# First stage of a decoder layer: six split and three raw weight parts, and the memory's values over 512 columns

## The chip, the core and the metric

The kernel runs on one NeuronCore of a Trainium2 chip. The metric is the device time of one execution in microseconds (us). The core's engines are PE (matrix products and transposes), DVE (vector), ACT (scalar and activation), POOL and SP; SP computes nothing and issues most of the DMA transfers, which 16 DMA engines carry out. Every engine, SP too, takes its instructions strictly in the order in which they stand in its queue.

## The reference

One decoder layer: a token-mixing sub-layer (RWKV-7 time mixing and a sparse attention, merged by gates), a cross-attention into 256 memory tokens, and a gated MLP, each followed by a LayerNorm. The parts that matter here are the input projection, the compression of the attention's keys and values, and the memory's keys and values:

```python
proj = x @ w_in[l]                       # x (1024, 1024)
...
def compress(t, pe, w1, w2):             # windows of 32 tokens, stride 16: 63 of them, 2 groups
    blk = t[:, cidx] + pe[None, None, :, None, :]
    blk = blk.transpose(0, 3, 1, 2, 4).reshape(B, G, n_cmp, CMP_BLOCK * dh)
    return jax.nn.gelu(blk @ w1) @ w2    # w1 (2048, 256), w2 (256, 64)
...
def memory_cross_attention(x, mem, wq, wk, wv, wo):
    k = (mem @ wk).reshape(B, M, X_HEADS, X_HEAD_DIM)    # mem (256, 1024), wk and wv (1024, 1024)
    v = (mem @ wv).reshape(B, M, X_HEADS, X_HEAD_DIM)
```

## The kernel before

**Products.** Every float32 operand of a large product is split into a high part and a low rest of the same size (`split`, L199): ACT writes the high part (L200), DVE subtracts it from the source (L201). `mm3` (L194) then makes three products per pair of tiles, high by high, high by low and low by high (L195 to L197), into one PSUM bank.

**Weights.** `wload` (L211) brings a weight block from HBM in parts of at most 1024 elements a partition, which is 512 KB: a part is four row tiles of 256 columns, two of 512, three of 280, eight of 128. For each part SP issues a DMA into a tile `raw` (L224), and `split` writes the tiles `wh` and `wl`. The three tiles of a part come from a pool that `in_turn` picks, in the first stage from `wa` and `p0` by turns. In each of the two pools one raw tile and two pairs of split tiles go round, so two raw and four split parts exist at a time; a new load waits until its raw tile has been split, a new split until the last product on its old tiles is done. From the second stage on only `wa` is left, or `wa` with another pool.

**The first stage** (up to L505) runs in this order: the projection of 512 columns for the selected and window branches' source (`nsa_proj`, L340) with its own weight loads (`wkv_split`, L290), in 8 token tiles of 24 products; the transpose of the memory (`mem_T`); one 256-column block of the memory's keys (`mem_k`, L445) and one of its values (`mem_v`, L455); the windows of the compressed keys; a projection of 280 columns; the compression of the keys (`compress`, L390), two halves of 1024 rows in 2 parts each; the second key and value block, the second one between the windows of the compressed values and their compression; the third key block; the query projection of 512 columns, in 4 parts; the third value block, the fourth key block, the fourth value block. The results of `mem_k` and `mem_v` go to DRAM (`kscr`, `vscr`) and are read again in the cross-attention.

A block of `mem_k` takes 48 products over 256 columns and 2 parts of weights, a block of `mem_v` the same; the keys have the weights as the stationary operand, the values have them as the moving one.

**After it.** `scope0.close()` ends the first stage and frees the pool `p0`; the next pool lies over it, each of its tiles waiting for what lay there. The next stage begins with projections (`prj`, `large` at L512) whose weights come through `wa` alone, beside the recurrence of RWKV, whose order on PE is written out by a small planner. PSUM banks are picked by `in_turn` as well, with one count for each role that goes on from stage to stage.

**Order of the queues.** The framework (Tile) puts the instructions of each engine in order when the kernel is built, by priority (mostly the order of the program) and by when it reckons that each can start, and sets the semaphores. SP's queue holds loads and stores in one order.

Of the kernel before, what the change touches and what calls it, by code (L numbers as in the profile page):

```python
# [10 lines left out]
F32 = mybir.dt.float32  # L11
F32R = mybir.dt.float32r
AF = mybir.ActivationFunctionType
# [5 lines left out]
P = 128  # L19
# [3 lines left out]
HALF = 512  # L23
# [103 lines left out]
def layer_kernel(ctx: ExitStack, tc, I, out, cst):  # L127
# [5 lines left out]
    cur = {}  # L133
    turn = {}

    def opened(name, side="left"):
        st = ExitStack()
        ctx.callback(st.close)
        return st, st.enter_context(tc.tile_pool(name=name, bufs=1, side=side, reuse_waits="tile"))

    def banks(name, **roles):

        if "psum" in cur:
            cur["psum"][0].close()
        st = ExitStack()
        ctx.callback(st.close)
        cur["psum"] = st, st.enter_context(tc.tile_pool(name=name, bufs=1, space=PSUM, reuse_waits="tile"))
        cur["banks"] = roles

    def stt(shape, dt=F32, name="st"):  # L150
        return cur["st"].tile(shape, dt, tag="st", name=name, bufs=cur["nst"])

    def b8(shape, dt=F32, name="b8"):
        if "plan" in cur:
            p, n = cur[next(cur["plan"])]
            return p.tile(shape, dt, tag="a8", name=name, bufs=n)
        return cur["b8"].tile(shape, dt, tag="a8", name=name, bufs=cur["n8"])

    def in_turn(key, xs):
        turn[key] = turn.get(key, -1) + 1  # L160
        return xs[turn[key] % len(xs)]
# [5 lines left out]
    def pg(name="pg"):  # L167
        return bank("g", name)
# [4 lines left out]
    def pst(name="pst"):  # L173
        return bank("t", name)
# [4 lines left out]
    V, S, G, PE, SP = nc.vector, nc.scalar, nc.gpsimd, nc.tensor, nc.sync  # L179

    ident = const.tile([P, P], F32, name="ident")
    _, wa = opened("wa", "right")
    x_scope, xp = opened("xp", "right")
    scope0, p0 = opened("p0")
    cur.update(st=p0, nst=4, b8=p0, n8=3, w=[wa, p0])
    banks("ps0", g=[0, 1, 2, 3], t=[4, 5, 6, 7])

    epsln = const.tile([P, 1], F32, name="epsln")
# [5 lines left out]
    def mm3(o, lh, ll, rh, rl, start, stop):  # L194
        PE.matmul(o, lh, rh, start=start, stop=False)  # L195
        PE.matmul(o, lh, rl, start=False, stop=False)  # L196
        PE.matmul(o, ll, rh, start=False, stop=stop)  # L197

    def split(src, h, l):  # L199
        S.activation(h, src, AF.Copy)  # L200
        V.tensor_sub(l, src, h.bitcast(F32))  # L201

    class W:
        def __init__(self, ku):
            self.ku, self.h, self.l = ku, [], []
# [5 lines left out]
    def wload(pieces, kt=8):  # L211

        n = sum(p.shape[1] for p in pieces)
        w = W(min(kt, WUNIT // n))
        for k0 in range(0, kt, w.ku):
            ku = min(w.ku, kt - k0)
            wp = in_turn("w", cur["w"])
            raw = wp.tile([P, ku, n], F32, tag="raw", bufs=1, name="raw")
            h = wp.tile([P, ku, n], F32R, tag="wh", bufs=2, name="wh")
            l = wp.tile([P, ku, n], F32R, tag="wl", bufs=2, name="wl")  # L220
            o = 0
            for p in pieces:
                m = p.shape[1]
                SP.dma_start(raw[:, :, o:o + m], p[k0 * P:(k0 + ku) * P].rearrange("(k p) n -> p k n", p=P))  # L224
                o += m
            split(raw, h, l)
            w.h.append(h)
            w.l.append(l)
        return w
# [23 lines left out]
    ps = pst("zz")  # L253
# [35 lines left out]

    def wkv_split(u):  # L290
        wp = in_turn("w", cur["w"])
        h = wp.tile([P, 2, HALF], F32R, tag="wh", bufs=2, name="wh")
        l = wp.tile([P, 2, HALF], F32R, tag="wl", bufs=2, name="wl")
        split(wraw[u // 2][:, 2 * (u % 2):2 * (u % 2) + 2], h, l)
        wkv.h.append(h)
        wkv.l.append(l)
# [13 lines left out]
    for gi, grp in enumerate(groups):  # L310
        n = sum(r for _, r in grp)
# [28 lines left out]
    def nsa_proj(cc, n, scale, nb, nh, w=None, ahead=lambda tt: None):  # L340
        w = w or wload([win[:, NSA0 + cc:NSA0 + cc + n]])
        for tt in range(NT):
            ahead(tt)
            ps = pg("np")
            gemmN(ps[:, :n], xT, tt, w, 0, n)
            t = stt([P, HALF], name="nst")
            S.activation(t[:, :n], ps[:, :n], AF.Copy, scale=scale)
            v = t[:, 0:256 * nb].rearrange("p (b h d) -> p b h d", h=4, d=64)[:, :, 0:nh, 0:16]
            for z in range(nb):
                vz = v[:, z]  # L350
                co = cso[:, tt * 16:tt * 16 + 16]
                si = cso[:, P + tt * 16:P + tt * 16 + 16]
                a = p0.tile([P, nh, 16], F32, name="rpa", tag="rpa", bufs=2)
                b = p0.tile([P, nh, 16], F32, name="rpb", tag="rpb", bufs=2)
                G.tensor_tensor(a, vz, bc(co, nh), op=OP.mult)
                G.tensor_tensor(b[:, :, 0:8], vz[:, :, 8:16], bc(si[:, 0:8], nh), op=OP.mult)
                G.tensor_tensor(b[:, :, 8:16], vz[:, :, 0:8], bc(si[:, 8:16], nh), op=OP.mult)
                G.tensor_tensor(vz, a, b, op=OP.add)
            SP.dma_start(rawn[tt * P:(tt + 1) * P, cc:cc + n], t[:, :n])
# [12 lines left out]
    def windows(cc, pe):  # L372
        blk = b8([P, 16, 2, 63], name="blk")
        for g in range(2):
            ev = p0.tile([P, 4, 2, 64], F32, name="ev", tag="ev", bufs=2)
            src = rawn[:, cc + g * 64:cc + g * 64 + 64].rearrange("(b e r) d -> e b r d", b=4, e=P, r=2)
            for b in range(4):
                SP.dma_start(ev[:, b], src[:, b])
            ps = pst("cT")
            for b in range(4):  # L380
                PE.transpose(ps[:, b * P:(b + 1) * P], ev[:, b].rearrange("p r d -> p (r d)"), ident)
            for q in range(2):
                V.tensor_tensor(blk[:, 8 * q:8 * q + 8, g, :], ps[:, 8 * q:8 * q + 504].rearrange("p (i b) -> p b i", b=8),
                                pv[:, col[pe] + 8 * q:col[pe] + 8 * q + 8][:, :, None].to_broadcast([P, 8, 63]), op=OP.add)
        bh = b8([P, 16, 126], F32R, "blkh")
        bl = b8([P, 16, 126], F32R, "blkl")
        split(blk.rearrange("p b g i -> p b (g i)"), bh, bl)
        return bh, bl
# [35 lines left out]
    vscr = drp.tile([MEM, D], F32, name="vscr")  # L424
    memh = p0.tile([P, 8, MEM], F32R, name="memh")
    meml = p0.tile([P, 8, MEM], F32R, name="meml")
# [18 lines left out]
    def mem_k(j):  # L445
        w = wload([I["xa_wk"][0][:, j * 256:(j + 1) * 256]])
        for q in range(2):
            ps = pg("mk")
            for k in range(8):
                mm3(ps[:, :MEM], *w.at(k, q * P, P), memh[:, k], meml[:, k], k == 0, k == 7)  # L450
            t = stt([P, MEM], name="mks")
            S.activation(t, ps[:, :MEM], AF.Copy)
            SP.dma_start(kscr[j * 256 + q * P:j * 256 + q * P + P, :], t)

    def mem_v(j):  # L455
        w = wload([I["xa_wv"][0][:, j * 256:(j + 1) * 256]])
        for mt in range(2):
            ms = slice(mt * P, mt * P + P)
            ps = pg("mv")
            for k in range(8):  # L460
                mm3(ps[:, :256], memh[:, k, ms], meml[:, k, ms], *w.at(k, 0, 256), k == 0, k == 7)
            t = stt([P, 256], name="mvs")
            S.activation(t, ps[:, :256], AF.Copy)
            SP.dma_start(vscr[ms, j * 256:(j + 1) * 256], t)

    def first(tt):
        if tt:
# [22 lines left out]

    mem_T()
    mem_k(0)
    mem_v(0)
    blocks = windows(512, "nsa_pe_k")
    nsa_proj(1024, 280, 1.0, 1, 2)
    compress(*blocks, "nsa_ck_w1", "nsa_ck_w2", True)
    mem_k(1)
    blocks_v = windows(640, "nsa_pe_v")
    mem_v(1)
    compress(*blocks_v, "nsa_cv_w1", "nsa_cv_w2", False)  # L500
    mem_k(2)
    nsa_proj(0, 512, 0.125, 2, 4)
    mem_v(2)
    mem_k(3)
    mem_v(3)  # L505


    gq = list(range(16))
# [441 lines left out]
    with tc.manual_schedule(engines={mybir.EngineType.PE}):  # L950
        while not all(t.done for t in outputs_):
            for tasks in classes:
                t = next((t for t in tasks if not t.done), None)
# [23 lines left out]
    for br, cc in enumerate((768, 1024)):  # L977
# [4 lines left out]
        for j in range(2):  # L982
            ps = pst("kT")
# [15 lines left out]
    for j in range(2):  # L999
        n = (C_ANY - C_CAU) // 2  # L1000
# [283 lines left out]
    w = dict(zip((2, 3), cur["wmb"]))  # L1284
# [20 lines left out]
    for j, k in todo:  # L1305
        g = gate_load(1, k, 0, lambda sh, name: stt(sh, name=name))
        ps = pg("mg")
# [117 lines left out]
    for h in range(XQ):  # L1425
        x_query(h)
        if h == 0:
            kvh = [b8([P, 2048], F32R, f"kvh{i}") for i in range(2)]
            kvl = [b8([P, 2048], F32R, f"kvl{i}") for i in range(2)]
            for i in range(2):  # L1430
                t = b8([P, 2048], name="kvld")
# [34 lines left out]
    for n in (2, 4, 4, 4, 4, 4):  # L1466
# [4 lines left out]
        for i in range(n):  # L1471
            w = wload([wup[:, (f + i) * P:(f + i + 1) * P], wup[:, FF + (f + i) * P:FF + (f + i + 1) * P]])
            gt = b8([P, 2, T], F32R, "gT")
            last = [sm.tile([P, 2], F32, name="cl", tag="cl", bufs=6) for _ in range(2)]
            for half in range(2):
                c = []
                for q in range(2):
                    ps = pg("up")
# [17 lines left out]
        if done:  # L1496
            w = [cols(0), cols(1)]
# [4 lines left out]
        else:  # L1502
            for j in range(2):
                w = cols(j)
# [30 lines left out]
```

## Time and profile before

| | us |
|---|---|
| timed runs, median of 3 | 2225.76 (2222.63 to 2226.09) |
| the profiled execution, its time | 2223.49 |
| its span in the trace | 2221.7 |
| PE busy in the span | 2131.7 (96%) |
| DVE busy | 1232.4 (55%) |
| ACT busy | 889.2 (40%) |

The span runs from the first to the last recorded instruction; what lies around it makes up the difference to the execution's time. The products of a full stream overlap: the profile draws each longer than the distance between two starts.

### The profile page before, as it was taken

The page shows a single profiled execution, that of the slowest core. Times are in us where ns is not written, and L with a number is a line of the kernel's source. Part 1 is how long each engine was busy: PE and PEld are TensorE (multiplying, and loading weights), DVE is VectorE, ACT ScalarE, POOL GpSimd, SP SyncE. Part 2 cuts the span into 40 slices and gives each one's busy share as a digit, 9 for nine tenths or more (in the row PEclk, how much of TensorE's full clock was granted, in tenths as well). Part 3 has the DMA queues.
Part 4 walks back from the last instruction along what each step waited for, and adds up shares of the span by engine and source line. Part 5 has one row for each costly group of instructions (what it writes and reads, how often), then busy time and mean ns, then how long its engine had stood idle before and what let it go on. Part 6 is the DMA issues. An engine that isn't in the chain of part 4 may idle for free.

```text
span 2221.7 us, 31651 instructions
## 1 busy us (share of the span) xinstructions
PE 2131.7 (96%) x12301; PEld 1706.0 (77%) x12301; DVE 1232.4 (55%) x2416; ACT 889.2 (40%) x1441; POOL 475.0 (21%) x544
## 2 busy tenths in 40 slices
PE   9989999999999899999899999999999999999997
PEld 7978777777778667756678877788888888888886
DVE  3422576777652787888656535275444434344447
ACT  3433443544533576776523424142322313132232
POOL 2112231333300244444422101030100101000013
PEclk9999999999999999999999999999999999999999
DMA  6544112121223321112252313111111111111102
GB/s 206 152 150 124 49 24 56 36 52 32 62 59 94 110 66 45 42 45 68 72 189 86 123 38 114 39 39 57 38 48 48 54 42 57 39 57 57 57 29 86
DMA packets 196659, 157.91 MB, mean 71 GB/s; under 512 B 49061, under 2 KB 164766, under 8 KB 196510
## 3 DMA queue, kind: packets, MB, share of 16 engines
q1 hardware_dynamic: 184798, 139.10, 21.2%
q10 hardware_dynamic: 11136, 14.68, 2.0%
q0 software_dynamic: 576, 2.10, 0.3%
q8 instruction: 98, 1.61, 0.3%
q14 instruction: 51, 0.42, 0.1%
HBM read 125.86 MB, written 29.98 MB: 70 GB/s over the span
## 4 chain that ended last, share of the span: by engine, by line
PE 47%; DVE 5%; ACT 2%; DMA 1%; issue 1%; POOL 0%; SPq 0%; ACTq 0%; DVEq 0%; POOLq 0%
PE up L196 7%; PE up L197 7%; PE up L195 7%; PE dn L195 4%; PE dn L197 4%; PE dn L196 4%; PE op L195 2%; PE op L197 1%; PE op L196 1%; PE xq L195 1%; PE xq L196 1%; PE xq L197 1%; DVE acc L1334 1%; ACT acc L1333 1%; DVE bs L1327 1%
## 5 line engine op out<-in xcount | busy, mean ns | idle before, releaser
L200 ACT ACTIVATE wh<-raw 128x1024 fp32r<-128x1024 f32 (+1 forms) x160 | 168.8, 1055 | 474.9 <-PE dn L197 138.1
L201 DVE TENSOR_TENSOR wl<-raw,wh 128x1024 fp32r<-128x1024 f32 (+1 forms) x160 | 198.1, 1239 | 282.5 <-ACT wh L200 281.5
L196 PE MATMUL up<-nTl,wh 128*128 128x512 f32 x704 | 276.5, 393 | 0.0
L197 PE MATMUL up<-nTh,wl 128*128 128x512 f32 x704 | 276.4, 393 | 0.0
L195 PE MATMUL up<-nTh,wh 128*128 128x512 f32 x704 | 276.4, 393 | 0.0
L1458 DVE SCALAR_TENSOR_TENSOR cv<-up,pv,cv 128x511 f32<-128x511 f32 (+1 forms) x176 | 131.5, 747 | 145.4 <-ACT cv L1456 143.4
L1482 POOL TENSOR_TENSOR cv<-cv 128x512 f32<-128x512 f32 x44 | 56.8, 1291 | 630.9 <-DVE cl L1462 413.5
L196 PEld LDWEIGHTS up<-nTl,wh 128*128 128x128 f32 x704 | 132.3, 188 | 29.6
L195 PEld LDWEIGHTS up<-nTh,wh 128*128 128x128 f32 x704 | 132.2, 188 | 29.6
L197 PEld LDWEIGHTS up<-nTh,wl 128*128 128x128 f32 x704 | 132.2, 188 | 29.6
L1106 POOL TENSOR_TENSOR pl<-pe,ph 128x512 fp32r<-128x512 f32 x87 | 114.3, 1317 | 161.3 <-ACT ph L1105 97.3
L195 PE MATMUL dn<-wh,gT 128*128 128x512 f32 x352 | 138.1, 393 | 0.2 <-ACT wh L200 0.2
L197 PE MATMUL dn<-wh,gT 128*128 128x512 f32 x352 | 137.5, 391 | 0.0
L196 PE MATMUL dn<-wl,gT 128*128 128x512 f32 x352 | 136.9, 389 | 0.0
L1493 DVE SCALAR_TENSOR_TENSOR acc<-acc,dn 128x512 f32<-128x512 f32 x96 | 65.5, 686 | 95.5 <-PE dn L197 94.9
L1456 ACT ACTIVATE cv<-up,pv 128x512 f32<-128x512 f32 x88 | 68.5, 778 | 117.2 <-PE up L197 117.2
L195 PE MATMUL gt<-xTh,wh 128*128 128x512 f32 x256 | 113.0, 441 | 0.5 <-DVE nm L1074 0.5
L197 PE MATMUL gt<-xTh,wl 128*128 128x512 f32 x256 | 102.3, 399 | 0.0
L196 PE MATMUL gt<-xTl,wh 128*128 128x512 f32 x256 | 101.9, 398 | 0.0
L1335 POOL TENSOR_TENSOR acc<-acc,lngb 128x1024 f32<-128x1024 f32 x21 | 50.4, 2401 | 206.0 <-DVE acc L1334 129.8
L1105 ACT ACTIVATE ph<-pe 128x512 fp32r<-128x512 f32 (+1 forms) x148 | 90.2, 627 | 6.9 <-POOL macc L1223 4.6
L195 PE MATMUL prj<-xTh,wh 128*128 128x512 f32 x208 | 90.5, 435 | 2.2 <-ACT wh L200 2.2
(365 smaller groups left out, 5092.2 us busy)
## 6 DMA issues: line engine op xcount, KB each, us to landing
raw<-in_ffn_w_up_dram SPq DMA_DIRECT2D x88, 256.0 KB
raw<-in_w_in_dram SPq DMA_DIRECT2D x33, 512.0 KB
raw<-in_ffn_w_down_dram SPq DMA_DIRECT2D x22, 512.0 KB
gscr<-gst ACTq DMA_DIRECT2D x32, 256.0 KB
rawn<-nst SPq DMA_DIRECT2D x16, 256.0 KB
raw<-in_xa_wk_dram SPq DMA_DIRECT2D x8, 512.0 KB
raw<-in_xa_wv_dram SPq DMA_DIRECT2D x8, 512.0 KB
gl<-gscr SPq DMA_DIRECT2D x16, 256.0 KB
```

The source lines that it names most:

```text
L195: PE.matmul(o, lh, rh, start=start, stop=False)
L196: PE.matmul(o, lh, rl, start=False, stop=False)
L197: PE.matmul(o, ll, rh, start=False, stop=stop)
L200: S.activation(h, src, AF.Copy)
L201: V.tensor_sub(l, src, h.bitcast(F32))
L1105: S.activation(h, e, AF.Copy)
L1106: in_turn("l", LTURN)(l, e, h.bitcast(F32), op=OP.subtract)
L1335: (V if tt == NT - 1 else G).tensor_tensor(r[:, c], r[:, c], gb[:, 1, c], op=OP.add)
L1456: S.activation(c, ps, AF.Identity, scale=pc("cw2", ci), bias=pc("ffn_conv_b", ci))
L1458: V.scalar_tensor_tensor(c[:, s:], ps[:, :HALF - s], pc(nme, ci), c[:, s:], op0=OP.mult, op1=OP.add)
L1482: G.tensor_tensor(c[0], c[0], c[1], op=OP.mult)
L1493: V.scalar_tensor_tensor(v, v, 1.0 if f else ALPHA, ps, op0=OP.mult, op1=OP.add)
```

## The change

In the first stage the weight parts are dealt out `p0`, `wa`, `p0` by turns. `p0` holds two raw tiles and four pairs of split tiles, `wa` one and two as before, so that three raw and six split parts exist at a time; `p0` grows by 20 KB a partition. `mem_v` works on 512 columns instead of 256: two calls of 48 products over 512 columns in place of four of 48 over 256, with 4 parts of two row tiles each. The order of the calls becomes: keys 0, keys 1, windows, projection of 280, compression of the keys, values 0, windows, compression of the values, keys 2, query projection, values 1, keys 3.

```diff
-    cur.update(st=p0, nst=4, b8=p0, n8=3, w=[wa, p0])
+    cur.update(st=p0, nst=4, b8=p0, n8=3, w=[p0, wa, p0])
...
+    def depth(wp):
+
+        return (2, 4) if wp is p0 else (1, 2)
...
-            raw = wp.tile([P, ku, n], F32, tag="raw", bufs=1, name="raw")
-            h = wp.tile([P, ku, n], F32R, tag="wh", bufs=2, name="wh")
-            l = wp.tile([P, ku, n], F32R, tag="wl", bufs=2, name="wl")
+            nr, ns = depth(wp)
+            raw = wp.tile([P, ku, n], F32, tag="raw", bufs=nr, name="raw")
+            h = wp.tile([P, ku, n], F32R, tag="wh", bufs=ns, name="wh")
+            l = wp.tile([P, ku, n], F32R, tag="wl", bufs=ns, name="wl")
...
-        h = wp.tile([P, 2, HALF], F32R, tag="wh", bufs=2, name="wh")
-        l = wp.tile([P, 2, HALF], F32R, tag="wl", bufs=2, name="wl")
+        h = wp.tile([P, 2, HALF], F32R, tag="wh", bufs=depth(wp)[1], name="wh")
+        l = wp.tile([P, 2, HALF], F32R, tag="wl", bufs=depth(wp)[1], name="wl")
...
-        w = wload([I["xa_wv"][0][:, j * 256:(j + 1) * 256]])
+        w = wload([I["xa_wv"][0][:, j * HALF:(j + 1) * HALF]])
...
-                mm3(ps[:, :256], memh[:, k, ms], meml[:, k, ms], *w.at(k, 0, 256), k == 0, k == 7)
-            t = stt([P, 256], name="mvs")
-            S.activation(t, ps[:, :256], AF.Copy)
-            SP.dma_start(vscr[ms, j * 256:(j + 1) * 256], t)
+                mm3(ps, memh[:, k, ms], meml[:, k, ms], *w.at(k, 0, HALF), k == 0, k == 7)
+            t = stt([P, HALF], name="mvs")
+            S.activation(t, ps, AF.Copy)
+            SP.dma_start(vscr[ms, j * HALF:(j + 1) * HALF], t)
...
     mem_k(0)
-    mem_v(0)
+    mem_k(1)
     blocks = windows(512, "nsa_pe_k")
     nsa_proj(1024, 280, 1.0, 1, 2)
     compress(*blocks, "nsa_ck_w1", "nsa_ck_w2", True)
-    mem_k(1)
+    mem_v(0)
     blocks_v = windows(640, "nsa_pe_v")
-    mem_v(1)
     compress(*blocks_v, "nsa_cv_w1", "nsa_cv_w2", False)
     mem_k(2)
     nsa_proj(0, 512, 0.125, 2, 4)
-    mem_v(2)
+    mem_v(1)
     mem_k(3)
-    mem_v(3)
```

## Rows read from the trace of the kernel before

**Rows 1.** The page, busy us, share of the span, instructions

```profile
PE 2131.7 (96%) x12301; PEld 1706.0 (77%) x12301; DVE 1232.4 (55%) x2416; ACT 889.2 (40%) x1441; POOL 475.0 (21%) x544
```

**Rows 2.** Windows: length, then busy PE, PEld, DVE, ACT, POOL, clock, DMA share, GB/s

```profile
54.70:70.00 15.30, 15.19 (x126) 14.48 (x125) 7.92 (x15) 7.39 (x12) 1.64 (x8) 1.00 0.61 179
...
95.00:139.50 44.50, 35.06 (x270) 31.59 (x269) 23.52 (x31) 22.49 (x34) 1.62 (x4) 1.00 0.57 174
...
184.70:204.80 20.10, 17.59 (x146) 17.16 (x144) 4.95 (x5) 7.56 (x12) 4.17 (x15) 1.00 0.58 180
...
205.00:2222.00 2017.00, 1942.72 (x11180) 1542.02 (x11179) 1163.39 (x2323) 812.87 (x1328) 433.31 (x374) 0.99 0.21 62
```

**Rows 3.** Timeline of PE: start, length, engine, line, output and inputs, shape

```profile
95.00 0.28 PE L195 MATMUL cm<-wh,blkh 128*126 128x256 f32 x1
...
139.53 0.40 PE L195 MATMUL np<-wh,xTh 128*128 128x512 f32 x1
...
184.72 0.28 PE L195 MATMUL mv<-wh,memh 128*128 128x256 f32 x1
...
190.43 0.29 PE L195 MATMUL mk<-memh,wh 128*128 128x256 f32 x1
...
204.77 0.50 PE L195 MATMUL prj<-xTh,wh 128*128 128x512 f32 x1 [2.20 <-ACT wh L200]
...
206.03 0.50 PE L197 MATMUL prj<-xTh,wl 128*128 128x512 f32 x1 [0.53 <-DVE wl L201]
```

**Rows 4.** Timeline of ACT, evictions of the query projection's last two token tiles

```profile
173.94 0.60 ACT L347 ACTIVATE nst<-np 128x512 f32<-128x512 f32 x1 [4.96 <-PE np L197]
179.50 0.60 ACT L347 ACTIVATE nst<-np 128x512 f32<-128x512 f32 x1 [4.96 <-PE np L197]
```

**Rows 5.** Groups of PE, 95.0 to 139.5: busy, mean ns, idle before

```profile
L381 PE MATMUL cT<-ident,ev 128*128 128x128 f32 x8 | 1.2, 272 | 0.0
...
L409 PE MATMUL kc<-hT,w2s 128*64 128x126 f32 x8 | 0.7, 283 | 0.0
```

**Rows 6.** Waits of PE, 95.0 to 139.5: us in total, times, longest

```profile
PE cm L196 <- DVE wl L201: 3.2, 5, 0.9
...
PE mk L195 <- ACT wh L200: 1.2, 2, 0.7
```

**Rows 7.** Timeline of ACT and SP, one part after another

```profile
123.56 1.06 ACT L200 ACTIVATE wh<-raw 128x1024 fp32r<-128x1024 f32 x1 [2.46 <-DMA raw<-in_nsa_cv_w_dram]
...
119.67 0.37 SPq L224 DMA_DIRECT2D raw<-in_nsa_cv_w_dram  x1
...
122.11 0.37 SPq L224 DMA_DIRECT2D raw<-in_nsa_cv_w_dram  x1
```

**Rows 8.** Timeline of ACT, DVE and SP, the next stage's first weights

```profile
203.66 1.06 ACT L200 ACTIVATE wh<-raw 128x1024 fp32r<-128x1024 f32 x1 [3.47 <-DMA raw<-in_w_in_dram]
...
196.88 1.22 DVE L201 TENSOR_TENSOR wl<-raw,wh 128x1024 fp32r<-128x1024 f32 x1 [1.23 <-ACT wh L200]
...
198.13 0.38 SPq L224 DMA_DIRECT2D raw<-in_w_in_dram  x1
```

**Rows 9.** Waits of SP's queue, 95.0 to 139.5

```profile
SPq L224 <- DVE wl L201: 16.1, 11, 2.4
```

**Rows 10.** Timeline of SP at the end of the 280-column projection

```profile
97.57 0.32 SPq L359 DMA_DIRECT2D rawn<-nst  x1
97.98 0.39 SPq L224 DMA_DIRECT2D raw<-in_xa_wk_dram  x1
```

**Rows 11.** Waits of PE, 205 to the end

```profile
PE x L860 <- DVE ZV L876: 7.6, 12, 1.4
PE z L871 <- ACT SV L867: 5.1, 7, 1.5
...
PE mg L195 <- ACT yh L200: 2.8, 1, 2.8
```

**Rows 12.** Window in the second compression, columns as in group 2

```profile
121.00:132.00 11.00, 6.49 (x44) 5.25 (x43) 4.75 (x4) 4.70 (x6) 0.00 (x0) 1.00 0.63 198
```

## Prediction

> **What bounds the kernel now.** I read the page first, then the table of windows, then the matrix engine's own timeline and waits. On the page the matrix engine PE is busy for 96% of the span [rows 1]; a change pays only where PE stands still or has less to do. The windows say where it stands still in the first stage, which fills the first 205 us of the trace: 44.5 us between 95.0 and 139.5 hold 35.06 us of PE work, and 20.1 us at the end hold 17.59, while the 15.3 us at its head are full but for 0.1; the granted clock is 1.00 in all three [rows 2]. The whole rest, 2017 us, has 1942.72 us of PE work in it and none of the changed lines [rows 2]. So what can be won lies in two places, and the clock is no part of it.
>
> A busy figure hides part of a stall, because one isolated matmul is drawn 0.28 to 0.4 us long while in a full stream the next one starts far earlier. I therefore count starts. 48 products over 256 columns take 190.43 - 184.72 = 5.71 us, 0.119 us each [rows 3]. Over 512 columns one token tile of 24 products takes 5.56 us, 0.232 us each: the eviction of each tile starts that long after the one before [rows 4].
>
> The first place runs from the first product of the first compression (95.00) to the first of the query projection (139.53), 44.53 us [rows 3]. It holds 96 products of the two compressions, 96 of two blocks of keys and 48 of one block of values, all over 256 columns: 240 x 0.119 = 28.6 us. The 28 small transposes and products beside them are drawn at 3.4 us together, four groups from 1.2 down to 0.7 [rows 5]. That makes 32.0 us of work, so 12.5 us of standing still. What PE waits for there is the split weights, the low half wl from DVE above all, and wh from ACT, in five rows from 3.2 down to 1.2 us, 9.4 together [rows 6].
>
> Why they are late: a part of 512 KB is issued by SP at 119.67, the next at 122.11, and the first one's split on ACT starts at 123.56 when it has landed, 3.9 us after its issue [rows 7]. The split takes 1.06 us on ACT and then 1.22 on DVE [rows 7, 8], and only then is the raw tile free for the next load; SP spends 16.1 us of this stretch before its loads on just that release [rows 9]. One raw tile so turns round in 3.9 + 1.06 + 1.22 = 6.2 us, and two of them give a part every 3.1 us. A compression uses up a part in 12 products, 1.43 us; a block of keys in 24, 2.9 us. The supply loses, part after part.
>
> The second place is the end. DVE finishes the low half of a late part at 198.1, SP issues the next stage's first weights at 198.13, they land at 203.66, and PE starts on them at 204.77, with another 0.53 us lost before 206.03 [rows 3, 8].
>
> **The change part by part.** *A third raw part and six split ones.* The parts are dealt out p0, wa, p0 now, and the first stage has 35 of them before and after (8 for the keys, 8 for the values, 4 + 3 + 4 for the projections, 8 for the compressions), so the later stages find the weight turn in the same place. I follow the buffers from the last projection tile before the first compression. Before, one part of the compression was split ahead by then and two lay raw. After, p0 has four split places of which the projection holds two, wa two of which it holds one: three parts are split ahead and three more lie raw, three parts more than before, or 9.3 us of the old supply. Those ready parts carry PE through the first compression (5.7 us) and into the values, and the rest has to arrive meanwhile: with three raw tiles at 6.2 us a turn, one every 2.07 us, against one every 1.4 to 2.9 us that PE uses.
>
> *The other order and the 512 columns.* Between the two compressions there is now one value block of 48 products at 0.232 us, 11.1 us, instead of a key and a value block of 5.7 each. It reads its four parts in its first half; the second half of 5.6 us needs no new part and lets the loads catch up. Following each part (its raw tile free, 3.9 us landing, a split place free, 2.3 us split), I find every later part ready one to six us before its turn; only the third and fourth value parts come out even or up to 1 us late, because their loads queue on SP behind the last projection store, which goes out at 97.57 with a load right behind it at 97.98 [rows 10]. I keep 1.0 us of stall here. The work is 96 + 48 products at 0.119 and 48 at 0.232, and the small ones: 17.1 + 11.1 + 3.4 = 31.7, with the stall 32.7 instead of 44.5: **-11.8 us**.
>
> *The end.* After the query projection come one value block (11.1) and one key block (5.7), 16.8 us, and then the next stage's first product; its third starts 0.5 later, at 17.3 us. Before, 206.03 - 184.72 = 21.3. The last key part is split some 4 us into this stretch, so the next stage's load is issued 13 us before it is wanted and needs 5.5 (198.13 to 203.66) plus the split. I keep 0.5 for the unknown: **-3.5 us**.
>
> *The head.* The second key block stands in the place of a value block with the same 48 products; PE is full there already [rows 2]: 0. *Fewer instructions.* The value products halve from 192 to 96 and their load instructions with them; 2 x 0.119 - 0.232 is 0.006 us each, 0.6 us in all, already inside the two sums. The evictions and stores of values fall from 8 to 4, off PE's path, on ACT and SP, which idle half of these stretches. *Where the bill could come later.* Four accumulations fewer (42 before, 38 after) in the rotation of PSUM banks leave two-bank stages in phase and shift three-bank ones by one; only the merge and what follows it use three. The merge's largest wait on inputs, not banks, is 2.8 us [rows 11], and I take 0, with 3 us either way for the range. p0 grows by 20 KB a partition, and the next stage lays tiles over it, but those are written first some 6 us after its first product: 0.
>
> Sum: -15.3 us. The profiled execution took 2223.5 us (span 2221.7), so 2208.2; the three timed runs lie higher, median 2225.8, and from there it is 2210.5. I say 2211.
>
> **A rule weighed.** In the stretch from 121 to 132 us the 16 DMA engines are busy 0.63 of the time and move 198 GB/s [rows 12], so at full share 314 GB/s and 1.7 us a part; three raw tiles ask for one every 2.07 us, inside that. The Trainium skill, in "DMA: Bandwidth & Descriptors", section "Issuing engines are not separate DMA queues", says that all transfers run on the same 16 engines and interleave with each other. By that rule alone a third load in flight only stretches the other two, and the time would be that of the first rival. The rows speak half against it: the load of 119.67, joined by another 2.4 us later, still landed in 3.9 [rows 7].
>
> **The rivals.** *Contention.* If landing grows with the loads in flight, 3.9 becomes 5.85, a turn 8.1, a part comes every 2.7 us. From 1 us after the first compression's start twelve parts have still to be loaded (the last of the query projection is wanted 32.4 us after that start): 1 + 12 x 2.7 + 2.3 = 35.7, 3.3 us of stall: gain 12, 2214. For it: two raw tiles alone keep the engines busy for 0.63 of the time, stores and all; against: a third one at the same rate asks for no more than they have left [rows 12].
>
> *Only the head start counts.* The third raw tile does nothing that lasts, because SP's queue (loads behind stores) or ACT's (splits behind evictions) keeps the old pace of 3.1: 1 + 12 x 3.1 + 2.3 = 40.5, 8 us of stall, gain 7, 2219. For it: SP is one queue in order, and loads do stand behind stores [rows 10]; against: 16.1 us of its waits are for the raw tile itself [rows 9].
>
> *No change.* The gain is given back in the bank phase of the merge or in another order of queues: within 4 us of 2226. Little speaks for it beyond the small waits of the later stages.
>
> *Slower.* The next stage is a recurrence of 64 steps whose PE order is written out, so it cannot step aside. PE waits there 7.6 us in 12 places for DVE's state update and 5.1 us in 7 for an ACT copy [rows 11]. The other engines' order is made anew with the changed first stage; if an ACT or DVE split of 1.06 to 1.22 us came ahead of that step's small copy, PE would wait this long. The gain of 15.3 and 4.5 more are used up at about 17 of the 64 steps, and at 20 of them it ends near 2234. Against it: the second stage's code, weights and pools are the same, and so should its order be.
>
> **How the numbers follow.** Forecast (gain 13 to 18) 0.56; contention 0.18; head start only 0.12; no change 0.08; slower 0.06. The forecast's own range is 2205 (neither of the two stalls that I kept, 1.5, the 3 us of the bank phase, and 1 for the spread of the runs, 2222.6 to 2226.1) to 2213. The other cases are taken in up to 2221, which leaves out no change and slower, 0.14, and some 0.05 below. 0.2% is 4.5 us, about what a measurement of this kernel can tell from none: the first three cases end below 2221.3, faster 0.86; same 0.08; slower 0.06.
>
> **What would show it.** In the profile after: from the first compression product to the first query product about 32.7 us; PE's waits for wl and wh in there fall from 9.4 us [rows 6] to 1 or 2; value products have one form, 128x512, 96 of them, 0.232 us apart; the next stage's first product starts near 189.5 without a wait for wh; and from there to the end it is 2017 us as before. Landings near 3.9 us with three loads in flight speak for the forecast, near 5.9 for contention; raw tiles that stay free while SP stands at a store, for the head start alone. The prediction is wrong if the stretch after the first stage is longer by more than 3 us, or if a wait for something else, the compression's input blocks or a bank, takes the weights' place.

## The result, and the profile after

| | before | after |
|---|---|---|
| timed runs, median | 2225.93 us (4 runs, 2222.63 to 2227.10) | 2209.68 us (4 runs, 2206.68 to 2211.47) |
| profiled execution, span in the trace | 2221.7 us | 2209.7 us |
| first product of the next stage | 204.77 us [rows 3] | 192.87 us |

The ratio is 0.9931, with a 95% interval of 0.9919 to 0.9944: 15 us faster, between 12.5 and 18. The two traces are 12.0 us apart, less than that interval: the profiled execution before (2223.49 us) lies 2.4 us under its median, the one after (2211.47 us) 1.8 above its own. What the granted clock (the share of PE's full 2.4 GHz that the chip lets it run at) has to do with it stands in the part on the prediction and in the last section.

The page says little, as before [rows 1]:

```profile
PE 2127.1 (96%) x12205; PEld 1698.6 (77%) x12205; DVE 1232.5 (56%) x2416; ACT 888.6 (40%) x1437; POOL 475.9 (22%) x544
```

The windows of the changed kernel, columns as in [rows 2]; the first three are the head, the stretch between the projections and the end of the first stage, the last is all that follows:

```profile
54.10:70.60 16.50, 15.08 (x123) 14.35 (x124) 7.09 (x16) 7.28 (x12) 1.61 (x8) 1.00 0.65 198
95.50:129.80 34.30, 31.34 (x212) 27.62 (x211) 22.96 (x28) 20.36 (x26) 2.64 (x4) 1.00 0.72 212
176.20:192.90 16.70, 16.70 (x98) 14.68 (x97) 3.56 (x3) 4.30 (x6) 2.00 (x8) 1.00 0.53 152
...
192.87:2209.70 2016.83, 1941.49 (x11182) 1540.71 (x11180) 1162.61 (x2322) 812.70 (x1329) 435.04 (x380) 0.99 0.21 62
```

The middle stretch went from 44.5 us with 9.4 idle to 34.3 with 3.0; the DMA engines' share rose from 0.57 to 0.72 in it, since the same parts come in less time. The end is full. The rest is as long as before, 2016.8 against 2016.9 (2221.7 - 204.77). All of the traced difference lies in the first stage.

PE's timeline, the starts that answer to [rows 3]:

```profile
95.54 0.28 PE L195 MATMUL cm<-wh,blkh 128*126 128x256 f32 x1
...
129.83 0.40 PE L195 MATMUL np<-wh,xTh 128*128 128x512 f32 x1
...
176.17 0.39 PE L195 MATMUL mv<-wh,memh 128*128 128x512 f32 x1
...
192.87 0.39 PE L195 MATMUL prj<-xTh,wh 128*128 128x512 f32 x1
...
193.34 0.40 PE L197 MATMUL prj<-xTh,wl 128*128 128x512 f32 x1
```

No wait stands before the next stage's first or third product now; before, these were 2.20 and 0.53 us [rows 3]. What PE still waits for from 95 to 130, against [rows 6]:

```profile
PE hT L407 <- ACT hid L402: 1.2, 1, 1.2
PE mk L197 <- DVE wl L201: 1.0, 2, 0.8
PE mk L195 <- ACT wh L200: 0.6, 1, 0.6
PE cm L197 <- DVE blkl L201: 0.2, 1, 0.2
```

Waits for split weights fell from 9.4 us to 1.6. A new one came up, for the hidden values of the compression, and it can be read on the timeline of ACT and PE:

```profile
101.55 1.28 ACT L402 ACT_TABLE_LOAD   x1 [0.45 <-PE cm L197]
...
102.84 0.38 ACT L402 ACTIVATE hid<-cm 126x256 f32<-126x256 f32 x1
103.28 0.20 PEld L407 LDWEIGHTS hT<-ident,hid 126*128 126x128 f32 x2 [1.63 <-ACT hid L402]
103.28 0.43 PE L407 MATMUL hT<-ident,hid 126*128 126x126 f32 x2 [1.20 <-ACT hid L402]
```

ACT loads another function table for 1.28 us before the Gelu; PE has three value products between the compression and the transposes of its result, and then stands. The Trainium skill, "ScalarE: Activation LUTs", section "What ACT_TABLE_LOAD costs", gives 1283 ns for the load, as here, and a drain of 1380 ns to it; this trace shows no time for it: ACT is idle for 0.45 us before the load, and the activation starts at 102.84, right behind it (101.55 + 1.28).

### The profile page after: what moved, and what is told of

Read it like the earlier page. It is cut to its first block, busy times and chain, and to the rows that moved or that the text cites. A ratio compares the mean times of both kernels' runs of the same rounds, so it can differ in the third digit from the quotient of the medians.

```text
span 2209.7 us, 31430 instructions
## 1 busy us (share of the span) xinstructions
PE 2127.1 (96%) x12205; PEld 1698.6 (77%) x12205; DVE 1232.5 (56%) x2416; ACT 888.6 (40%) x1437; POOL 475.9 (22%) x544
## 4 chain that ended last, share of the span: by engine, by line
PE 46%; DVE 5%; ACT 2%; DMA 1%; issue 1%; POOL 1%; SPq 0%; ACTq 0%; DVEq 0%; POOLq 0%
PE up L196 7%; PE up L195 7%; PE up L197 7%; PE dn L195 4%; PE dn L197 3%; PE dn L196 3%; PE op L195 1%; PE op L197 1%; PE op L196 1%; PE xq L195 1%; PE xq L196 1%; PE xq L197 1%; DVE acc L1337 1%; ACT acc L1336 1%; DVE wl L201 1%
```

## Experiments

In each, the start of the next stage's first product in the trace tells the first stage by itself; the kernel before has it at 204.77, the changed kernel at 192.87. From 50 us on to there, both ran at a granted clock of 1.00 throughout. Eight of the other traces have 3.4 or 6.8 us at 1.2 GHz in this part, in one piece or two. In such a piece PE's work takes nearly twice as long (in e8, products over 256 columns start 0.21 us apart instead of 0.119), so that it costs up to half its length; the table lists them, since they move the starts. Each began during or just after waits of PE of about 1 to 4 us; not every such wait brings one (2.20 us before 204.77 in the kernel before did not). The ratios are of the runs timed beside the kernel before on the same chip.

| run | what | first product of the next stage, us | at 1.2 GHz from 50 us to there, us | median us | ratio, 95% interval |
|---|---|---|---|---|---|
| e1_buffers | buffers alone | 192.60 | 0 | 2209.85 | 0.9937 (0.9917 to 0.9958) |
| e2_order | order and 512 columns alone | 203.94 | 3.4 | 2225.22 | 0.9998 (0.9984 to 1.0013) |
| e3_split6_raw2 | two raw, six split | 203.81 | 6.8 | 2217.82 | 0.9977 (0.9965 to 0.9989) |
| e4_split5_raw3 | three raw, five split | 196.61 | 3.4 | 2214.09 | 0.9958 (0.9943 to 0.9974) |
| e5_256 | values over 256 columns | 192.54 | 0 | 2210.32 | 0.9936 (0.9923 to 0.9950) |
| e6_raw4 | four raw | 194.48 | 3.4 | 2211.46 | 0.9938 (0.9921 to 0.9954) |
| e7_memT | memory transposed earlier | 192.22 | 0 | 2210.08 | 0.9935 (0.9918 to 0.9951) |
| e8_tails | ends of the compressions later | 197.04 | 6.8 | 2212.04 | 0.9941 (0.9922 to 0.9959) |
| e9_all | e6, e7 and e8 together | 193.97 | 6.8 | 2210.48 | 0.9937 (0.9923 to 0.9952) |
| e10_windows | e7, second windows earlier | 192.25 | 3.4 | 2207.84 | 0.9917 (0.9901 to 0.9932) |
| e11_best | e10 and the later ends | 191.69 | 3.4 | 2209.12 | 0.9929 (0.9916 to 0.9941) |

### Buffers or order

**e1_buffers** takes the change's pools and leaves `mem_v` and the order of the calls as before.

```diff
-    cur.update(st=p0, nst=4, b8=p0, n8=3, w=[wa, p0])
+    cur.update(st=p0, nst=4, b8=p0, n8=3, w=[p0, wa, p0])
...
+        return (2, 4) if wp is p0 else (1, 2)
```

> Only the buffers: parts dealt p0, wa, p0 with three raw and six split, the order of the calls and the 256-column values as before. Theory (the supply of parts bounds the first stage, and the third raw part raises its rate): nearly all of the gain, 11 to 15 us under the kernel before, the next stage's first product near 194 us, the stretch from the first compression product to the first query product near 33 to 35 us instead of 44.5. Rival (the order gives PE something to do while parts arrive): at most a third, 5 us, the stretch near 40.

**e2_order** is the other half: the new `mem_v` over `HALF` columns and the new order, over the pools as before.

```diff
     mem_k(0)
-    mem_v(0)
+    mem_k(1)
...
-        w = wload([I["xa_wv"][0][:, j * 256:(j + 1) * 256]])
+        w = wload([I["xa_wv"][0][:, j * HALF:(j + 1) * HALF]])
```

> Only the order of the calls and the 512-column values, two raw and four split parts as before. Theory: the same parts at the same 3.1 us each must arrive between the two projections, so the stretch stays within 2 us of 44.5 and the time within 3 us of before. Rival (order): 6 to 10 us faster than before, the stretch 35 to 39.

PE's timeline in e1_buffers, the first products of the query projection and of the next stage:

```profile
131.09 0.39 PE L195 MATMUL np<-wh,xTh 128*128 128x512 f32 x1
...
192.60 0.40 PE L195 MATMUL prj<-xTh,wh 128*128 128x512 f32 x1
```

and in e2_order:

```profile
137.82 0.40 PE L195 MATMUL np<-wh,xTh 128*128 128x512 f32 x1
...
203.94 0.41 PE L195 MATMUL prj<-xTh,wh 128*128 128x512 f32 x1
```

The first compression starts at 95.55 and 94.53 in these, so the stretch is 35.5 us with the buffers alone (33 to 35 expected) and 43.3 with the order alone. e1 has the whole gain, 12.2 us of the 11.9; e2 has 0.8 (up to 1.7 more at full clock, since its piece at 1.2 GHz lies at 189.0), and its time is that of before within 0.2%. PE's waits in the stretch say the same, first e1, then e2:

```profile
PE hT L407 <- ACT hid L402: 2.4, 2, 1.4
PE cm L197 <- DVE blkl L201: 0.6, 1, 0.6
PE mk L195 <- ACT wh L200: 0.2, 1, 0.2
```

```profile
PE cm L196 <- DVE wl L201: 3.3, 5, 0.9
PE mv L196 <- DVE wl L201: 2.4, 4, 1.4
PE cm L195 <- ACT wh L200: 1.6, 2, 1.0
```

With the buffers the split weights are waited for 0.2 us in the old order and 1.6 in the new; without them the new order waits 8.4 in all, on the same names as before. The rival, that the order gives PE something to do meanwhile, falls.

### Raw tiles or split tiles

**e3_split6_raw2** and **e4_split5_raw3** change the pool's depth in the changed kernel. In e3 `wa` and `p0` also take turns, as before, since with one raw tile in each pool thirds would load `p0` with two parts of three.

e3:

```diff
-    cur.update(st=p0, nst=4, b8=p0, n8=3, w=[p0, wa, p0])
+    cur.update(st=p0, nst=4, b8=p0, n8=3, w=[wa, p0])
...
-        return (2, 4) if wp is p0 else (1, 2)
+        return (1, 4) if wp is p0 else (1, 2)
```

e4:

```diff
-        return (2, 4) if wp is p0 else (1, 2)
+        return (2, 3) if wp is p0 else (1, 2)
```

> The changed kernel with one raw tile in p0 instead of two, and parts dealt wa, p0 by turns: six split, two raw. Theory (rate of the raw tiles): each pool's raw tile still turns round in about 6.2 us for every second part, so the stretch is 41 to 45 us and the time 0 to 4 us under before. Rival (only the head start counts): the parts split ahead are what helps, 6 to 9 us under before, the stretch 35 to 38.

> The changed kernel with three pairs of split tiles in p0 instead of four: three raw, five split. Theory (rate): the rate stays, one part less lies ahead; the stretch 34 to 36.5 us, within 2 us of the changed kernel's 34.3. Rival (only the head start counts): 3 us or more longer than the changed kernel.

PE's timeline, the next stage's first product in e3:

```profile
203.81 0.50 PE L195 MATMUL prj<-xTh,wh 128*128 128x512 f32 x1
```

and in e4, with PE's largest wait there between 95 and 131 us:

```profile
196.61 0.40 PE L195 MATMUL prj<-xTh,wh 128*128 128x512 f32 x1
```

```profile
PE mk L195 <- ACT wh L200: 2.5, 1, 2.5
```

The pace at which SP sends out loads follows the raw tiles. From the first compression's start to the query projection's weights a load goes out every 3.3 us in the kernel before, every 3.2 to 3.3 in e2 and e3 (two raw tiles), and every 2.5 in the changed kernel, e1 and e4 (three), whatever the split tiles and the order.

e3's stretch says nothing by itself: its first compression starts only at 100.24 (95.54 in the changed kernel), since the projection of 280 waited 2.3 us for its weights and then ran 3.4 us at 1.2 GHz, and PE makes six products of the query projection, from 130.44 on, ahead of the rest of the second compression. By the next stage's start e3 gains 1.0 us of the 11.9, up to 3.4 more at full clock; its timed runs gain 2 to 8. The nearer comparison is e2, which has two raw tiles, the new order and the 512 columns as well, and four split parts: its next stage starts at 203.94 against 203.81, and its median is 2225.22 against 2217.82. In the traces the two further split parts are so worth at most 3.5 us without the third raw tile (203.94 less 203.81 - 3.4). That is a part of the gain; between the 0 to 4 us of the theory and the 6 to 9 of the rival the timed runs do not decide.

With the third raw tile, the sixth split pair is worth 3.7 us, where I had expected at most 2; up to 1.7 of that is the clock's (piece at 121.0). e4's stretch is 39.1 us (134.74 - 95.64), not the 34 to 36.5 of the theory: one part fewer lies ready when the first compression starts, and the shortage comes out later, at the key block. So the rate alone was not the whole theory. The raw tile sets how fast parts come, the split tiles how many of them can wait for PE, and the head start that the prediction counted (a part is some 3.1 us of supply) is real.

### How far the supply is from its limit

The landings in the changed kernel, on the timelines of SP and ACT, three loads after the first compression began:

```profile
96.15 0.38 SPq L229 DMA_DIRECT2D raw<-in_xa_wv_dram  x1
...
99.55 0.39 SPq L229 DMA_DIRECT2D raw<-in_xa_wv_dram  x1
100.03 0.44 SPq L229 DMA_DIRECT2D raw<-in_nsa_cv_w_dram  x1
...
121.14 0.37 SPq L229 DMA_DIRECT2D raw<-in_w_in_dram  x1
...
100.04 1.06 ACT L200 ACTIVATE wh<-raw 128x1024 fp32r<-128x1024 f32 x1 [2.78 <-DMA raw<-in_xa_wv_dram]
...
103.97 1.06 ACT L200 ACTIVATE wh<-raw 128x1024 fp32r<-128x1024 f32 x1 [0.75 <-DMA raw<-in_xa_wv_dram]
...
105.58 1.06 ACT L200 ACTIVATE wh<-raw 128x1024 fp32r<-128x1024 f32 x1 [0.55 <-DMA raw<-in_nsa_cv_w_dram]
```

The load that goes out alone lands in 3.9 us, the next two, issued 0.5 us apart, in 4.4 and 5.6. From 96.15 to 121.14 eleven loads went out, one every 2.5 us; before, fifteen from 95.61 to 142.22, one every 3.3. By the semaphores' updates in the traces (the signals that a transfer has landed) the eleven landed in 3.5 to 5.5 us, 4.5 on average, the fifteen in 3.4 to 5.4, 3.8 on average. The forecast had a pace of 2.07, contention 2.7. The Trainium skill's rule that all transfers run on the same 16 engines and interleave ("DMA: Bandwidth & Descriptors", section "Issuing engines are not separate DMA queues") agrees with these longer landings, and yet the third load in flight pays.

**e6_raw4** puts a third raw tile into `p0`, deals `p0`, `wa`, `p0`, `p0`, and makes room by letting the warm-up tile share the staging buffers.

```diff
-    cur.update(st=p0, nst=4, b8=p0, n8=3, w=[p0, wa, p0])
+    cur.update(st=p0, nst=4, b8=p0, n8=3, w=[p0, wa, p0, p0])
...
-    zz = p0.tile([P, HALF], F32R, name="zz")
+    zz = p0.tile([P, HALF], F32R, tag="st", bufs=4, name="zz")
...
-        return (2, 4) if wp is p0 else (1, 2)
+        return (3, 4) if wp is p0 else (1, 2)
```

> The changed kernel with a fourth raw part (three in p0, dealt p0, wa, p0, p0; the warm-up tile shares the staging buffers to make room). If three raw parts already cover what PE uses: within 1.5 us of the changed kernel in the first stage, what is left of the waits for split weights (2.8 us) going at most. If the DMA engines were the limit (contention): landings of 5 us and more with four in flight, and no gain or a loss. If the supply were still short: 2 us or more off the first stage.

The next stage starts at 194.48, later than without. 0.8 us of the 1.6 are lost before the first compression (96.31 against 95.54), where the memory's transposes wait 2.0 us for DVE; from there it is 98.2 against 97.3, with up to 1.7 us lost to the clock (piece at 120.6). The waits for split weights in the stretch stay, 1.4 against 1.6, so no gain of a fourth raw part is shown. Why not stays open. SP's four loads in a row, and one of ACT's splits after them:

```profile
101.30 2.25 SPq L229 DMA_DIRECT2D raw<-in_nsa_cv_w_dram  x4
...
111.58 1.06 ACT L200 ACTIVATE wh<-raw 128x1024 fp32r<-128x1024 f32 x1 [0.78 <-PE mv L197]
```

The four landed in 4.0, 5.1, 6.0 and 6.8 us, which is the sign that I had named for the DMA engines as the limit. But ACT's split at 111.58 waited for PE to finish with an old split tile and not for a landing, so the six split tiles may be the limit as well. No run has four raw parts with more split tiles.

**e5_256** gives the values two blocks of 256 columns again, in the place of one of 512.

```diff
-        w = wload([I["xa_wv"][0][:, j * HALF:(j + 1) * HALF]])
+        w = wload([I["xa_wv"][0][:, j * 256:(j + 1) * 256]])
...
     mem_v(0)
+    mem_v(1)
...
-    mem_v(1)
+    mem_v(2)
+    mem_v(3)
```

> The changed kernel with the values over 256 columns again, two blocks one after the other where one block of 512 stands: the same buffers, the same order. Theory (buffers and their rate are the whole of it): 0.6 us more product time, the next stage's first product 0.3 to 1.5 us later than in the changed kernel (192.9). Rival (the second half of a 512-column block, which needs no new part, is what lets the loads catch up): 3 us or more later.

It started its first compression 1.2 us later than the changed kernel (96.77) and still had its next stage at 192.54, 0.3 earlier. Of the theory the 0.6 us of product time are there at most, and they are outweighed: PE waits for no split weight in the stretch, where the changed kernel waits 1.6. That two 256-column blocks give their split tiles back earlier, where one block of 512 keeps all four parts until its second half, would do it; no run shows it by itself. The second half, which the prediction counted on to let the loads catch up, is not needed.

### What is left

Five runs went for the last 3 to 4 us. **e7_memT** moves the memory's transposes before the last token tile of the first projection.

```diff
         if tt:
             x_split(tt)
+            if tt == 7:
+                mem_load()
+                mem_T()
             return
```

> The changed kernel with the memory loaded and transposed before the last token tile of the first projection instead of after it, so that its split no longer stands in ACT's queue behind weight splits while PE waits. Theory: PE's wait for memh (1.3 us) and the idle time around the transposes go: the first key product about 3 us earlier after the projection's end, the next stage 1.5 to 3 us earlier. Rival: PE waits for something else there, the key weights, and the next stage starts within 0.5 us of the changed kernel.

The first compression starts 1.5 us earlier (94.00) and the next stage 0.65: the rest went into weights further on, wh 1.1 us instead of 0.6 for the key block and 0.5 instead of none for the query projection.

**e8_tails** splits `compress` after the Gelu and calls its second half behind the next memory block.

```diff
-    compress(*blocks, "nsa_ck_w1", "nsa_ck_w2", True)
+    hid = compress(*blocks, "nsa_ck_w1")
     mem_v(0)
+    compressed(hid, "nsa_ck_w2", True)
...
-    compress(*blocks_v, "nsa_cv_w1", "nsa_cv_w2", False)
+    hid = compress(*blocks_v, "nsa_cv_w1")
     mem_k(2)
+    compressed(hid, "nsa_cv_w2", False)
```

> The changed kernel with the second half of each compression (transposes of the hidden values, the small products) called one block of memory products later, so that PE does not wait for the activation and its table load. Theory: PE's 1.2 us wait for hid goes and about as much that the second compression loses: next stage 1.5 to 2.5 us earlier. Rival: the wait is covered by another one behind it (weights for the values or keys), under 0.5 us.

The wait for hid is gone and the stage ends 4.2 us later. PE's longest wait in its stretch:

```profile
PE mk L197 <- DVE wl L201: 4.0, 1, 4.0
```

DVE's timeline before that product, and the window behind the wait:

```profile
117.32 0.21 DVE L421 TENSOR_TENSOR KLc<-kc,KHc 64x63 fp32r<-64x63 f32 x1 [0.79 <-ACT KHc L420]
...
119.32 0.23 DVE L421 TENSOR_TENSOR KLc<-kc,KHc 64x63 fp32r<-64x63 f32 x1 [1.20 <-ACT KHc L420]
...
120.16 2.35 DVE L201 TENSOR_TENSOR wl<-raw,wh 128x1024 fp32r<-128x1024 f32 x2
```

```profile
120.20:127.10 6.90, 5.67 (x26) 5.67 (x27) 4.48 (x4) 1.88 (x1) 0.00 (x0) 0.51 0.49 152
```

The rival was right in kind: a few calls moved, and in DVE's queue the moved second half's small steps, waiting for ACT, now stand ahead of the split of the key block's low half. Then the clock was at half until 127.07, where PE's products over 256 columns start 0.21 us apart instead of 0.119: working from 121.43 on, PE lost up to 2.8 us more by it. **e9_all**, with e6 and e7 as well, ends between.

> The fourth raw part, the early memory transpose and the late compression ends together. If their gains add: next stage 3.5 to 6 us earlier than in the changed kernel, time 2204 to 2207 where the changed kernel has 2209.7. If they share one wait: 2 to 3 us.

It came out at 193.97; up to 3.4 us of that is the clock's (6.8 us from 117.1 on), which would still leave it short of the 3.5 to 6 us: the gains do not add, and are at best the 2 to 3 us of one shared wait. **e10_windows** makes the second windows' call before the first value block, so that PE runs the second compression ahead of the key block, in the order in which their weights are loaded; **e11_best** has the later ends too.

```diff
-    mem_v(0)
     blocks_v = windows(640, "nsa_pe_v")
+    mem_v(0)
```

> The early memory transpose, and the windows of the compressed values called before the first value block instead of after it, so that the second compression can run as soon as its weights are there and the key block behind it no longer runs first with weights that come later. Theory (what is left are the waits for that key block's weights, 2.1 us): they go, the next stage's first product near 190 us. Rival (they are supply still short, in whatever order): another product waits, 191.5 or later.

> As the run with the early windows, and the second half of each compression one block later too. Theory: also without the wait for the hidden values (1.2 us), the next stage's first product near 189, time about 3.5 us under the changed kernel. Rival: the queue of loads is ordered otherwise and a wait for weights takes its place, as in the run that moved these halves alone.

In both all waits for split weights are gone, and neither starts the next stage where it was expected; each has one piece at 1.2 GHz (at 126.1 and 115.8), which cost up to 1.7 us, so that at full clock they might have come near 190.5 and 190.0 (estimates). e10 waits 4.0 us for hid in two places instead of 1.2; in e11, from 50 to 192 us, all that PE waits for is this:

```profile
PE kc L417 <- DVE hT L412: 2.2, 1, 2.2
PE vc L426 <- DVE hT L412: 1.3, 1, 1.3
```

a small copy on DVE between the transposes and the small products of a compression. The copy takes 0.4 us; it is late because it stands in DVE's queue behind weight splits (in the first case with four short steps between):

```profile
110.93 3.49 DVE L201 TENSOR_TENSOR wl<-raw,wh 128x1024 fp32r<-128x1024 f32 x3
...
114.92 0.36 DVE L412 COPY hT<-hT 128x252 f32<-128x252 f32 x1
...
129.60 1.23 DVE L201 TENSOR_TENSOR wl<-raw,wh 128x1024 fp32r<-128x1024 f32 x1 [1.51 <-ACT wh L200]
130.86 0.42 DVE L412 COPY hT<-hT 128x252 f32<-128x252 f32 x1
```

e11's trace has the shortest first stage, 1.2 us under the changed kernel, e10 the lowest time; their intervals overlap the changed kernel's, so no version here is shown to beat it.

## Why the prediction was right

*The time.* 2211 was forecast from the runs' median and 2209.68 measured, and the gain of 15.3 us in the sum lies within what the timed runs show (12.5 to 18). That it fits so well is in part luck. In the traces the next stage starts 11.9 us earlier, at 192.87 and not near the 189.5 forecast. The changed kernel's four runs had a granted clock of 0.990 on average; of the 39 runs of the kernel before that were timed beside the experiments (0.988 on average) the eight at 0.990 or 0.991 took 2221.7 us on average, which is 12.3 above those four (2209.4). So an estimate of the gain at equal clock is 12 us, and the terms of the sum were some 3 us too large.

*The bound.* The first stage was supply-bound at the two places named: e1 takes nearly all waits for split weights away with buffers alone, and e2 with the order alone keeps them.

*The stretch.* Forecast 32.7 us, -11.8; measured 129.83 - 95.54 = 34.3, -10.2. The one us of weights' wait that I kept came out at 1.6, but at a key block; for the third and fourth value parts, where I had put it, PE waits for nothing. What was left out is the compressions' own chain, the table load, the Gelu and the copy, 1.2 us here; it is the wait for something else that I had named as a sign of being wrong, but small beside the 7.8 us of weights' waits that went. The query projection took over part of the second chain: from its first product to the value block's it takes 46.3 us instead of 45.2, so -9.1 in all.

*The end.* Forecast -3.5; from the value block to the third product of the next stage 193.34 - 176.17 = 17.2 against 21.3, -4.1. The 0.5 us kept for the unknown were not needed.

*The head.* Forecast 0; the memory's split on ACT stands behind a weight split that the new buffers let start early, and PE waits 1.3 us for it, the only wait of PE from 50 to 95 us:

```profile
55.71 0.90 ACT L200 ACTIVATE wh<-raw 128x840 fp32r<-128x840 f32 x1 [0.85 <-DMA raw<-in_w_in_dram]
56.52 2.04 ACT L200 ACTIVATE memh<-mT 128x512 fp32r<-128x512 f32 x4
```

```profile
PE mk L195 <- ACT memh L200: 1.3, 1, 1.3
```

In the kernel before, PE waits for nothing there; e7, which moves the memory ahead, has no such wait either. The first compression starts 0.5 us later than before (95.54 against 95.00). That is the bill of the deeper prefetch that I did not see: a split that is ready sooner also stands in ACT's queue sooner.

*512 columns and order.* I gave the second half of the value block a part in closing the gap. e2 (the old buffers) and e1 and e5 (the new ones) show no measurable worth of order or columns.

*Contention and head start.* The forecast kept the landing at 3.9 us with three loads in flight; it came out at 4.5 on average, between that and contention's 5.85, and the pace at 2.5, nearer to that rival's 2.7 than to the forecast's 2.07. The stretch of 34.3 us also lies between the two, 32.7 and 35.0 (31.7 + 3.3), and the 12 us of the traces are what that rival gave. So contention was there in part; its 3.3 us of stall were not, PE waits 1.6 for split weights. The second rival's head start is a part of the gain (e4, 2.0 to 3.7 us) and not all of it (e3).

*What follows the stage.* Shifted and otherwise unchanged: 2016.8 us against 2016.9, the recurrence's waits 7.4 and 5.1 us against 7.6 and 5.1 [rows 11]. Neither the bank phase nor another order of queues brought a bill that can be seen.

## What to carry to other kernels

Follow one buffer around: issue, landing, both halves of the split, release. The turn divided by the number of buffers is the pace, and where it is slower than use, a further raw buffer pays and a new order does not; the deeper store behind it adds a few us (e4), and by itself made up for only a part (e3). When the large wait is gone, the small chains beside it (a table load, a copy that stands behind splits in its engine's queue) set what is left, and moving calls for them can lay the queues worse. Before two traces are compared by a start in them, look at the clock up to there: a few us at half of it hide a gain.

## What the runs showed of the hardware

The stretch after the first stage is the same work in all thirteen traces and lasted from 2010.2 us (e4) to 2019.5 (e1). Much of that is the granted clock of PE. One window of e1 and the same of e4, where about the same work lies:

```profile
960.00:980.00 20.00, 18.75 (x86) 11.68 (x85) 14.23 (x30) 13.89 (x27) 11.21 (x10) 0.91 0.24 62
```

```profile
960.00:980.00 20.00, 18.34 (x89) 11.29 (x87) 14.59 (x33) 14.82 (x28) 11.14 (x10) 1.00 0.24 61
```

The engine load is nearly the same, and in one execution the clock is granted in full, in the other 3.4 us of the window run at 1.2 GHz. I summed (1 - granted clock) x length over the stretch, from each trace's records of the clock: from 17.2 us (e4 and e9) to 26.1 (e1), 24.2 before and 22.4 after. Less this sum, the stretch lasts 1991.1 to 1995.1 us, a spread of 4.0 instead of 9.3. So differences of a few us between single executions of this kernel say little unless the clock is beside them.

The timed runs, which spread by 1.6 to 11.6 us within one kernel, go with the clock as well: of the 39 runs of the kernel before, the eight at a granted clock of 0.990 or 0.991 took 2219.07 to 2225.26 us, the seven at 0.986 or less 2226.17 to 2229.72. Why one execution is granted more than another no run shows.
